# The opening of a decoder-layer kernel: smaller first pieces on two DMA queues, another warming operand, and five additions on another engine

## The chip, the cores and the metric

The kernel runs on one core of a Trainium2 chip. The metric is device time in microseconds (us) for one execution. The core has TensorE (PE, with its weight loads shown apart as PEld), VectorE (DVE), ScalarE (ACT), GpSimd (POOL) and SyncE (SP), which here only issues DMAs. Its DMAs are moved by 16 DMA engines.

## The reference

One decoder layer on x of 1024 tokens by 1024 features, in float32. What matters for the change is the head of it:

```python
h = rms_norm(x, norm1_w[l])
proj = h @ w_in[l]
da_q, da_k, da_v, dn_qkv, dn_z, dn_a, dn_b = jnp.split(proj, [SPLIT_1, ..., SPLIT_6], axis=-1)
```

`rms_norm` divides each token by the root of its mean square and multiplies with a weight per feature. The columns of `proj` feed a differential attention and a gated delta rule, which run in parallel over the same tokens. Their outputs are concatenated, projected and added to x, and a squared-ReLU MLP with its own norm follows.

## The kernel before, in words

A float32 product is made of three products of rounded parts. Each operand is split into a part H, rounded to a shorter mantissa, and the rest L = value - H. A product is then H·H + H·L + L·H, on one PSUM bank. ACT makes the H parts and DVE the L parts.

**The first stage** computes 520 columns of `proj` (the gate columns z, with a and b) and needs the whole of x. x lies in `x_cols`, feature by feature: block `k` (of `KB` = 8) has 128 features on the partitions and 1024 tokens. The stage walks over k. For every k it multiplies each of `NT` = 8 token blocks `tb` with 260 weight columns (`UC`), in three terms "h", "l" and "m", so 24 matmuls of 128x260 for each k, into eight PSUM banks `zb`. The weights of this first half (called unit 1) come as four raw pieces of two k each (`wraw`, loaded by `z_weights`). After the walk, `second(tb)` makes the other 260 columns (unit 0) and PE goes on to the next projections.

The work of each k, by name and line of the kernel before:

- `load_x` (L288) loads block k of x into `xt`, five buffers deep; `z_weights` (L280) loads a raw weight piece. All go through SP's queue, in an order that the code writes out, and the ninth DMA and each later one waits until the DMA eight places before it has landed.
- `x_round` (L302, ACT) makes `hH` from `xt` times the norm weights `n1c` (a small load, L275); `x_rest` (L305, DVE) makes `hL`.
- `z_round` (L309, ACT) makes `wH` of a weight piece; `z_rest` (L313, DVE) makes `wL`.
- `square` (L340, ACT) squares block k, and `add_square` (L343, DVE) adds it to `ssum_` (`xsum` in the trace), from which the norm factors follow. Squares use three buffers (`nsq`).
- `z_mm` issues the matmuls: L320 is "h", L322 "l", L324 "m".

The norm factor of a token is only applied after the products, so the matmuls needn't wait for the sums of squares. PE reads them at L402, after `second(0)`: 8 float32 products of `ssum_` with the tile `ones`.

**What sets the order.** In this stage the order on PE, DVE and ACT is that of the code (a manual schedule): k by k. Behind it only PE's order is fixed, and a scheduler places the rest. Ahead of the first data, PE runs `WARM` = 19 transposes of the identity `ident` (L351), which GpSimd builds with a memset and a select (masks.py:197 and 199). Their results are not used.

Of the kernel before, what the change touches and what calls it, by code (L numbers as in the profile page):

```python
# [9 lines left out]
F32 = mybir.dt.float32  # L10
# [3 lines left out]
ALU = mybir.AluOpType  # L14
# [4 lines left out]
P = 128  # L19
# [9 lines left out]
UC = 260  # L29


WARM = 19
MARGIN = 0.25
MIX_T = 8000.0
MIX_A = 3400.0
# [82 lines left out]
def tile_hymba_layer(  # L118
# [6 lines left out]
    nc = tc.nc  # L125
# [97 lines left out]
    V.memset(neghalf, -0.5)  # L223
    poshalf = const.tile([P, 4], F32, name="poshalf")
    V.memset(poshalf, 0.5)

    def rstd(o, ss, scale, eps, pool, tag, n):
        t = pool.tile([P, n], F32, tag=tag, name=tag) if pool else laid(tag)
# [42 lines left out]
    v4 = lambda t: t.rearrange("p (c d) -> p c d", d=P)  # L271
    ones = n1.tile([P, P], F32, name="ones")
    V.memset(ones, 1.0)
    n1c = n1.tile([P, KB], F32, name="n1c")
    nc.sync.dma_start(n1c, n1_cols)  # L275
    xts, wz = [], [[[staged(t).rearrange("p (k c) -> p k c", k=KB) for t in ("wH", "wL")], []] for _ in range(2)][::-1]

    def z_weights(u, i):
        raw = n2.tile([P, 2 * UC], F32, tag="wraw", name="wraw", bufs=8).rearrange("p (k c) -> p k c", k=2)
        last = nc.sync.dma_start(raw, w_in_v[:, 2 * i:2 * i + 2, 3072 + UC * u:3072 + UC * (u + 1)])  # L280
        wz[u][1].append(raw)
        return last

    def load_x(k, cuts=(slice(0, 1024),)):
        if cuts[0].start == 0:
            xts.append(n2.tile([P, SEQ], F32, tag="xt", name="xt", bufs=5))
        for c in cuts:
            nc.sync.dma_start(xts[k][:, c], x_cols[k, :, c])  # L288

    cut = (slice(0, 512), slice(512, 1024))  # L290
    load_x(0, cut[:1])
    z_weights(1, 0)
    load_x(0, cut[1:])
    for k in range(1, KB):
        load_x(k)
        if k in (1, 3, 5):
            z_weights(1, (k + 1) // 2)
    for i in range(4):
# [5 lines left out]
    def x_rest(k, c):  # L304
        V.scalar_tensor_tensor(hL[:, k, c], xts[k][:, c], n1c[:, k:k + 1], hH[:, k, c].bitcast(F32),  # L305
                               ALU.mult, ALU.subtract)

    def z_round(u, i):
        S.copy(wz[u][0][0][:, 2 * i:2 * i + 2], wz[u][1][i])  # L309

    def z_rest(u, i):
        wh, wl = [x[:, 2 * i:2 * i + 2] for x in wz[u][0]]
        V.tensor_tensor(wl, wz[u][1][i], wh.bitcast(F32), ALU.subtract)  # L313

    def z_mm(ps, u, tb, k, terms="hlm"):
        (wh, wl), _ = wz[u]
        sl = slice(tb * P, (tb + 1) * P)
        for t in terms:
            if t == "h":
                T.matmul(ps[:, :UC], hH[:, k, sl], wh[:, k, :], start=(k == 0), stop=False)  # L320
            elif t == "l":
                T.matmul(ps[:, :UC], hH[:, k, sl], wl[:, k, :], start=False, stop=False)  # L322
            else:
                T.matmul(ps[:, :UC], hL[:, k, sl], wh[:, k, :], start=False, stop=(k == KB - 1))  # L324
# [13 lines left out]
    def square(k):  # L338
        sqs[k] = n2.tile([P, SEQ], F32, tag="nsq", name="nsq", bufs=3) if k else ssum_
        S.activation(sqs[k], xts[k], AF.Square)  # L340

    def add_square(k):
        V.tensor_tensor(ssum_, ssum_, sqs[k], ALU.add)  # L343

    with tc.manual_schedule(engines={T.engine, V.engine, S.engine}):
        zb = [pool.tile([P, 512], F32, tag=tag, name="ps_z")
              for pool, tag in ((pj, "pj"), (ph, "ph"), (pm, "pm"), (pt_, "pt")) for _ in range(2)]
        first_table = n1.tile([P, 1], F32, name="first_table")
        S.activation(first_table, neghalf[:, 0:1], AF.Tanh)
        for i in range(WARM):  # L350
            T.transpose(zb[7][:, :P], ident, ident)  # L351
        for c in cut:
            x_round(0, c)
            if c.start == 0:
                z_round(1, 0)
        x_rest(0, cut[0])
        z_rest(1, 0)
        x_rest(0, cut[1])
        for t in "hlm":
            for tb in range(NT):  # L360
                z_mm(zb[tb], 1, tb, 0, t)
        square(0)
        for k in range(1, KB):
            x_round(k, full)
            if k % 2 and k < 7:
                z_round(1, (k + 1) // 2)
            elif k in (6, 7):
                z_round(0, k - 6)
            square(k)
            x_rest(k, full)  # L370
            if k % 2 and k < 7:
                z_rest(1, (k + 1) // 2)
            elif k in (6, 7):
                z_rest(0, k - 6)
            if 1 < k < 6:
# [12 lines left out]

    tail = zb[7]
# [1418 lines left out]
```

## Time and profile before

| what | value |
|---|---|
| median of 3 runs | 1230.07 us (1228.01 to 1232.25) |
| profiled execution, its time | 1229.3 us |
| its span (first to last record) | 1227.6 us |
| PE busy | 1211.4 us, 99% |
| DVE busy | 844.4 us, 69% |
| ACT busy | 609.9 us, 50% |
| GpSimd busy | 122.8 us, 10% |

A row of the timeline gives the start in us from the span's start, the duration in us, the engine, the line, the operation, what is written and read with its shape, and how often; brackets hold the idle time just before on that engine and what ended it. Several rows of one kind in a run are merged (x4). A matmul's end is modelled, and successive ones overlap: the spacing of starts says how fast PE goes. Sizes of DMAs are in KB of 1024 bytes.

### The profile page before, as it was taken

What the parts mean: (1) busy time and instruction counts of PE and PEld (TensorE: products, weight loads), DVE (VectorE), ACT (ScalarE), POOL (GpSimd) and SP (SyncE); (2) the same over time, 40 slices, a digit from 0 to 9 for tenths busy, and PEclk for the clock granted to TensorE, in tenths of its full rate; (3) what the DMA queues carried; (4) which work ended last, traced back from release to release, by engine and by line L of the source; (5) the groups of instructions that cost most, each with busy time, mean ns of one, the idle gap of its engine ahead of it and who ended that gap; (6) DMA issues with size and microseconds to landing.
All of it is one profiled execution on the core that took longest, in us unless ns stands there. A gap on an engine that the chain in (4) does not pass through costs nothing.

```text
span 1227.6 us, 17618 instructions
## 1 busy us (share of the span) xinstructions
PE 1211.4 (99%) x6331; PEld 1027.0 (84%) x6331; DVE 844.4 (69%) x1437; ACT 609.9 (50%) x1181; POOL 122.8 (10%) x162
## 2 busy tenths in 40 slices
PE   9999999999899999999999999999999999999998
PEld 9978888898788878888788888888888888888887
DVE  7686788477867567766798554565577955786553
ACT  8465545245567555656566444454563333333331
POOL 0011110223332331212100000000000000000000
PEclk9999999999999999999999999999999999999999
DMA  6554342457755674334528433443279855433301
GB/s 230 180 169 134 110 131 86 117 180 225 234 155 165 194 236 140 109 86 144 181 87 280 158 127 138 172 172 137 103 248 351 324 187 183 164 103 104 137 35 69
DMA packets 160784, 199.04 MB, mean 162 GB/s; under 512 B 20961, under 2 KB 120633, under 8 KB 160697
## 3 DMA queue, kind: packets, MB, share of 16 engines
q1 hardware_dynamic: 160696, 197.92, 49.0%
q8 instruction: 50, 0.82, 0.3%
q14 instruction: 38, 0.30, 0.1%
HBM read 132.32 MB, written 65.56 MB: 161 GB/s over the span
## 4 chain that ended last, share of the span: by engine, by line
PE 87%; DVE 4%; DMA 4%; ACT 2%; issue 2%; POOL 0%; SPq 0%; ACTq 0%; DVEq 0%; POOLq 0%
PE X L1406 5%; PE X L1405 5%; PE X L1407 5%; PE X L1723 4%; PE X L1721 4%; PE X L1722 4%; PE ps_dn L204 3%; PE ps_dn L206 3%; PE ps_dn L205 3%; PE Y L1406 3%; PE Y L1405 3%; PE Y L1407 3%; PE ps_qk L974 2%; PE ps_qk L976 2%; PE ps_qk L975 2%; PE Z L1723 2%
## 5 line engine op out<-in xcount | busy, mean ns | idle before, releaser
L1324 ACT CAST hH<-ur 128x1024 fp32r<-128x1024 f32 x56 | 58.7, 1050 | 166.0 <-PE X L1722 79.7
L1325 DVE TENSOR_TENSOR hL<-ur,hH 128x1024 fp32r<-128x1024 f32 x56 | 68.4, 1222 | 79.1 <-ACT hH L1324 79.0
L1325 DVE TENSOR_TENSOR op<-raw,op 128x1024 fp32r<-128x1024 f32 x48 | 58.7, 1223 | 75.7 <-PE X L1406 42.3
L1721 PE MATMUL X<-hH 128*128 128x512 f32 x224 | 87.1, 389 | 0.0
L1722 PE MATMUL X<-hL,hH 128*128 128x512 f32 x224 | 87.1, 389 | 0.0
L1723 PE MATMUL X<-hH,hL 128*128 128x512 f32 x224 | 87.1, 389 | 0.0
L974 PE MATMUL ps_qk<-wH,hH 128*128 128x512 f32 x192 | 81.2, 423 | 0.0
L204 PE MATMUL ps_dn<-hH,wH 128*128 128x512 f32 x192 | 76.0, 396 | 0.0
L205 PE MATMUL ps_dn<-hL,wH 128*128 128x512 f32 x192 | 75.6, 394 | 0.0
L976 PE MATMUL ps_qk<-wH,hL 128*128 128x512 f32 x192 | 75.5, 393 | 0.0
L206 PE MATMUL ps_dn<-hH,wL 128*128 128x512 f32 x192 | 75.4, 393 | 0.0
L975 PE MATMUL ps_qk<-wL,hH 128*128 128x512 f32 x192 | 75.1, 391 | 0.0
L1325 DVE TENSOR_TENSOR hL<-dw,hH 128x1024 fp32r<-128x1024 f32 x56 | 68.1, 1217 | 3.2 <-ACT hH L1324 3.2
L1324 ACT CAST op<-raw 128x1024 fp32r<-128x1024 f32 x48 | 50.5, 1052 | 34.7 <-PE Y L1407 20.1
L1324 ACT CAST hH<-dw 128x1024 fp32r<-128x1024 f32 x56 | 58.6, 1047 | 16.7 <-DMA dw<-in_w_down_dram 5.2
L1116 ACT ACTIVATE pexp<-ps_sc,mx 128x128 f32<-128x128 f32 (+7 forms) x64 | 47.3, 742 | 27.4 <-DVE mx L1112 27.3
L562 DVE SCALAR_TENSOR_TENSOR cy<-cp,pv,cy 128x512 f32<-128x512 f32 x72 | 53.8, 748 | 8.7 <-ACT cy L560 7.8
L1112 DVE TENSOR_REDUCE mx<-ps_sc 128x1 f32<-128x128 f32 (+7 forms) x64 | 47.7, 753 | 13.7 <-PE ps_sc L1110 13.0
L1244 PE MATMUL ps_op<-wH,hH 128*128 128x512 f32 x128 | 53.6, 419 | 0.0
L198 ACT CAST wH<-wraw 128x512 fp32r<-128x512 f32 x64 | 37.1, 623 | 27.6 <-DMA wraw<-in_w_in_dram 17.4
L1246 PE MATMUL ps_op<-wH,hL 128*128 128x512 f32 x128 | 50.4, 393 | 0.0
L1245 PE MATMUL ps_op<-wL,hH 128*128 128x512 f32 x128 | 50.0, 391 | 0.0
(355 smaller groups left out, 3391.1 us busy)
## 6 DMA issues: line engine op xcount, KB each, us to landing
ur<-ud SPq DMA_DIRECT2D x28, 1024.0 KB, 4.9
raw<-in_w_up_dram SPq DMA_DIRECT2D x32, 512.0 KB, 3.8
dw<-in_w_down_dram SPq DMA_DIRECT2D x32, 512.0 KB, 7.3
qk_d<-qa SPq DMA_DIRECT2D x32, 256.0 KB, 3.2
ud<-ua SPq DMA_DIRECT2D x16, 512.0 KB, 4.0
ud<-s SPq DMA_DIRECT2D x16, 512.0 KB, 2.7
wraw<-in_w_in_dram SPq DMA_DIRECT2D x24, 256.0 KB, 3.6
wraw<-in_w_in_dram SPq DMA_DIRECT2D x48, 128.0 KB, 2.6
```

The costliest lines, as they stand in the source:

```text
L204: T.matmul(ps, lh(k), rh(k), start=(k == 0), stop=False)
L205: T.matmul(ps, lh(k), rl(k), start=False, stop=False)
L206: T.matmul(ps, ll(k), rh(k), start=False, stop=(k == n - 1))
L974: T.matmul(ps, hH[:, 4 * kh + k, sl], wh[:, k, :], start=(kh + k == 0), stop=False)
L975: T.matmul(ps, hH[:, 4 * kh + k, sl], wl[:, k, :], start=False, stop=False)
L976: T.matmul(ps, hL[:, 4 * kh + k, sl], wh[:, k, :], start=False, stop=(kh + k == 4))
L1324: S.copy(dst[0], src)
L1325: V.tensor_tensor(dst[1], src, dst[0].bitcast(F32), ALU.subtract)
L1405: T.matmul(ps, op[0][:, k, cs], h[0][:, k, :], start=start and k == 0, stop=False, skip_group_check=True)
L1721: T.matmul(o, v[0][:, j, sl], v[2][:, j, c], start=s0, stop=False, skip_group_check=True)
L1722: T.matmul(o, v[0][:, j, sl], v[3][:, j, c], start=False, stop=False, skip_group_check=True)
L1723: T.matmul(o, v[1][:, j, sl], v[2][:, j, c], start=False, stop=s1, skip_group_check=True)
```

## The change

1. The first block of x comes as pieces of 256, 256 and 512 columns in place of two of 512; the second block comes as two of 512 in place of one of 1024. `n1c` is issued after the first piece of x in place of ahead of it.
2. The first raw weight piece (two k) is loaded as two halves of one k each. The half for k = 0 is issued by ACT's queue, ahead of ACT's other work, and the half for k = 1 by SP, behind both halves of x's second block. Rounding and rest of this piece are split in the same way.
3. PE's products before the data are 9 float32 matmuls of `ones` with itself, in place of 19 transposes of `ident`. `ones` is DVE's first memset; the memsets of `neghalf` and `poshalf` come behind it.
4. Of the additions of squares, those of blocks 1 to 5 go to GpSimd, and 6 and 7 stay on DVE, behind the walk.

```diff
-WARM = 19
+WARM = 9
...
     neghalf = const.tile([P, 32], F32, name="neghalf")
-    V.memset(neghalf, -0.5)
     poshalf = const.tile([P, 4], F32, name="poshalf")
-    V.memset(poshalf, 0.5)
...
     V.memset(ones, 1.0)
+    V.memset(neghalf, -0.5)
+    V.memset(poshalf, 0.5)
     n1c = n1.tile([P, KB], F32, name="n1c")
-    nc.sync.dma_start(n1c, n1_cols)
...
-    cut = (slice(0, 512), slice(512, 1024))
+    cut = (slice(0, 256), slice(256, 512), slice(512, 1024))
     load_x(0, cut[:1])
-    z_weights(1, 0)
+    first_raw = n2.tile([P, 2 * UC], F32, tag="wraw", name="wraw", bufs=8).rearrange("p (k c) -> p k c", k=2)
+    wz[1][1].append(first_raw)
+    nc.scalar.dma_start(first_raw[:, 0], w_in_v[:, 0, 3072 + UC:3072 + 2 * UC])
+    nc.sync.dma_start(n1c, n1_cols)
     load_x(0, cut[1:])
+    load_x(1, (slice(0, 512), slice(512, 1024)))
+    nc.sync.dma_start(first_raw[:, 1], w_in_v[:, 1, 3072 + UC:3072 + 2 * UC])
     for k in range(1, KB):
-        load_x(k)
+        if k > 1:
+            load_x(k)
...
-    def z_round(u, i):
-        S.copy(wz[u][0][0][:, 2 * i:2 * i + 2], wz[u][1][i])
+    def z_round(u, i, ks=slice(0, 2)):
+        S.copy(wz[u][0][0][:, 2 * i:2 * i + 2][:, ks], wz[u][1][i][:, ks])
...
     def add_square(k):
-        V.tensor_tensor(ssum_, ssum_, sqs[k], ALU.add)
+        (G if k < 6 else V).tensor_tensor(ssum_, ssum_, sqs[k], ALU.add)
...
         for i in range(WARM):
-            T.transpose(zb[7][:, :P], ident, ident)
+            T.matmul(zb[7][:, :P], ones, ones, start=True, stop=True)
         for c in cut:
             x_round(0, c)
             if c.start == 0:
-                z_round(1, 0)
-        x_rest(0, cut[0])
-        z_rest(1, 0)
-        x_rest(0, cut[1])
+                z_round(1, 0, slice(0, 1))
+        z_rest(1, 0, slice(0, 1))
+        for c in cut:
+            x_rest(0, c)
         for t in "hlm":
             for tb in range(NT):
                 z_mm(zb[tb], 1, tb, 0, t)
+        half = (slice(0, 512), slice(512, 1024))
+        for c in half:
+            x_round(1, c)
+            if c.start == 0:
+                z_round(1, 0, slice(1, 2))
         square(0)
         for k in range(1, KB):
-            x_round(k, full)
+            if k > 1:
+                x_round(k, full)
...
             square(k)
-            x_rest(k, full)
+            if k > 1:
+                x_rest(k, full)
+            else:
+                x_rest(1, half[0])
+                z_rest(1, 0, slice(1, 2))
+                x_rest(1, half[1])
...
-            if 1 < k < 6:
+            if 1 < k < 7:
                 add_square(k - 1)
...
-        for k in (5, 6, 7):
+        for k in (6, 7):
             add_square(k)
```

The order of PE's instructions changes in one row only, the products before the data. Three other places move. The first is ACT's queue from the program's start to the rounding of block 2. In these rows 128x520 is a weight piece for two k and 128x260 for one; `xsum` and `nsq` are written by `square`. Before:

```order
L349 ACT_TABLE_LOAD
L349 ACTIVATE first_table<-neghalf 128x1
L302 ACTIVATE hH<-xt,n1c 128x512
L309 CAST wH_76<-wraw 128x520
L302 ACTIVATE hH<-xt,n1c 128x512
L340 ACTIVATE xsum<-xt 128x1024
L302 ACTIVATE hH<-xt,n1c 128x1024
L309 CAST wH_76<-wraw 128x520
L340 ACTIVATE nsq<-xt 128x1024
```

and with the change:

```order
L293 DMA wraw<-in_w_in_dram 128x260
L354 ACT_TABLE_LOAD
L354 ACTIVATE first_table<-neghalf 128x1
L307 ACTIVATE hH<-xt,n1c 128x256
L314 CAST wH_76<-wraw 128x260
L307 ACTIVATE hH<-xt,n1c 128x256
L307 ACTIVATE hH<-xt,n1c 128x512 x2
L314 CAST wH_76<-wraw 128x260
L307 ACTIVATE hH<-xt,n1c 128x512
L345 ACTIVATE xsum<-xt 128x1024
L314 CAST wH_76<-wraw 128x520
L345 ACTIVATE nsq<-xt 128x1024
```

In both, the rounding of block 2 (128x1024) stands right behind the square of block 1 (the first `nsq`). The first square (`xsum`) stood between the two blocks of x, ahead of the rounding of block 1; it now stands behind that rounding and behind the second weight half.

The second place is SP's queue at the program's start, each row one DMA, with what it waits for (DMAHW are the completions of earlier DMAs). Before:

```order
L275 DMA n1c<-in_n_cols_dram 128x8
L288 DMA xt<-in_x_cols_dram 128x512
L280 DMA wraw<-in_w_in_dram 128x2x260
L288 DMA xt<-in_x_cols_dram 128x512
L288 DMA xt<-in_x_cols_dram 128x1024
L280 DMA wraw<-in_w_in_dram 128x2x260
L288 DMA xt<-in_x_cols_dram 128x1024 x2
L280 DMA wraw<-in_w_in_dram 128x2x260 [waits DMAHW0_49]
```

and with the change:

```order
L287 DMA xt<-in_x_cols_dram 128x256
L294 DMA n1c<-in_n_cols_dram 128x8
L287 DMA xt<-in_x_cols_dram 128x256
L287 DMA xt<-in_x_cols_dram 128x512 x3
L297 DMA wraw<-in_w_in_dram 128x260
L279 DMA wraw<-in_w_in_dram 128x2x260 [waits DMAHW0_49]
L287 DMA xt<-in_x_cols_dram 128x1024 [waits DMAHW1_49]
L287 DMA xt<-in_x_cols_dram 128x1024 [waits DMAHW2_49]
```

The weight half for k = 1 is now the seventh DMA of SP, behind all of blocks 0 and 1 of x, and the first DMA that waits for a completion is the one behind it.

The third place is GpSimd, between its constants (`tri`, `after`, `blk`) and the norm factors (`rt`), with the change:

```order
L433 AFFINE_SELECT tri<-ones 128x128
L267 AFFINE_SELECT after<-after 128x128
L552 AFFINE_SELECT blk<-blk 128x128
L348 TENSOR_TENSOR xsum<-xsum,nsq 128x1024 x5
L422 TENSOR_TENSOR rt<-nrt,neghalf 128x8
```

Before, `rt` follows `blk` directly. DVE has five additions fewer in the walk or behind it, and the squares of blocks 4 to 7 on ACT wait for GpSimd's additions, which give their buffers free, where they waited for DVE's.

More of the change, by code (lines that the diff above doesn't have):

```diff
@@ L306, in x_rest, with z_rest @@
                                ALU.mult, ALU.subtract)
-    def z_round(u, i):
[L309 to L313, printed above, removed]
+    def z_round(u, i, ks=slice(0, 2)):
+        S.copy(wz[u][0][0][:, 2 * i:2 * i + 2][:, ks], wz[u][1][i][:, ks])
+    def z_rest(u, i, ks=slice(0, 2)):
+        wh, wl = [x[:, 2 * i:2 * i + 2][:, ks] for x in wz[u][0]]
+        V.tensor_tensor(wl, wz[u][1][i][:, ks], wh.bitcast(F32), ALU.subtract)
     def z_mm(ps, u, tb, k, terms="hlm"):
```

## The prediction

> **What bounds the kernel now.** I read the page's busy times first, then the chain of waits and the timeline of the first 13 us, because all that the change edits runs before 33 us.
>
> ```profile
> span 1227.6 us, 17618 instructions
> PE 1211.4 (99%) x6331; PEld 1027.0 (84%) x6331; DVE 844.4 (69%) x1437; ACT 609.9 (50%) x1181; POOL 122.8 (10%) x162
> ...
> 12.00:16.00 4.00, 4.00 (x36) 4.00 (x35) 3.81 (x4) 4.00 (x6) 0.00 (x0) 1.00 1.05 378
> 16.00:20.00 4.00, 4.00 (x36) 4.00 (x35) 4.00 (x5) 4.00 (x5) 0.00 (x0) 1.00 1.05 356
> ```
>
> PE is busy for 99% of the span, and the stages from 12 to 20 us (their columns: stretch, length, PE, PEld, DVE, ACT, GpSimd, clock, DMA share, GB/s) show it full. So the change can only move the time at which PE begins to run without a gap. The chain of waits names that point (start, duration, what):
>
> ```profile
> 2.70 5.77 DMA xt<-in_x_cols_dram
> 8.49 1.16 ACT hH L302
> 9.70 0.39 PE ps_z L320
> ```
>
> Block 1 of x lands at 8.49, ACT rounds it, PE starts k = 1 at 9.70 and does not stop again in this stage. The timeline gives PE's side of it:
>
> ```profile
> 1.68 4.32 PE L351 MATMUL ps_z<-ident 128*128 128x128 f32 x19 [1.68 <-POOL ident masks.py:199]
> 5.86 0.76 PE L320 MATMUL ps_z<-wH,hH 128*128 128x260 f32 x4
> 6.92 0.75 PE L320 MATMUL ps_z<-wH,hH 128*128 128x260 f32 x4 [0.29 <-ACT hH L302]
> 8.46 1.12 PE L324 MATMUL ps_z<-wH,hL 128*128 128x260 f32 x8
> 11.72 1.12 PE L324 MATMUL ps_z<-wH,hL 128*128 128x260 f32 x8
> 12.68 0.28 PE L320 MATMUL ps_z<-wH,hH 128*128 128x260 f32 x1
> ```
>
> Starts in full flow are 0.12 us apart ((12.68 - 11.72) / 8), so a k of 24 matmuls takes 2.88 us. Products of k = 2 begin at 12.68. **That is the number to beat**: an earlier start of k = 0 is worth nothing unless k = 2 starts earlier too. All that PE could win is the wait ahead of 5.86 and the two gaps before 9.70.
>
> **ACT's queue.** It feeds each k, and its rows show what stands ahead of k = 2:
>
> ```profile
> 4.06 0.72 ACT L302 ACTIVATE hH<-xt,n1c 128x512 fp32r<-128x512 f32 x1 [1.76 <-DMA xt<-in_x_cols_dram]
> 5.18 0.63 ACT L309 CAST wH<-wraw 128x520 fp32r<-128x520 f32 x1 [0.40 <-DMA wraw<-in_w_in_dram]
> 6.14 0.72 ACT L302 ACTIVATE hH<-xt,n1c 128x512 fp32r<-128x512 f32 x1 [0.33 <-DMA xt<-in_x_cols_dram]
> 6.77 1.04 ACT L340 ACTIVATE xsum<-xt 128x1024 f32<-128x1024 f32 x1
> 8.49 1.15 ACT L302 ACTIVATE hH<-xt,n1c 128x1024 fp32r<-128x1024 f32 x1 [0.67 <-DMA xt<-in_x_cols_dram]
> 9.55 0.61 ACT L309 CAST wH<-wraw 128x520 fp32r<-128x520 f32 x1
> 10.06 1.06 ACT L340 ACTIVATE nsq<-xt 128x1024 f32<-128x1024 f32 x1
> 11.03 1.13 ACT L302 ACTIVATE hH<-xt,n1c 128x1024 fp32r<-128x1024 f32 x1
> ```
>
> The square of block 0 (6.77) runs inside the wait for block 1, so it is free. The rounding of block 2 ends at 12.16, half a microsecond before PE needs it. ACT is thus nearly the bound already.
>
> **The change, part by part.**
>
> *PE before the data.* `ones` is ready after one memset of DVE, where `ident` waits for two GpSimd instructions:
>
> ```profile
> 0.88 0.09 DVE L223 MEMSET neghalf<- 128x32 f32 x1 [0.88 <-PEq L1790]
> 0.96 0.17 DVE L273 MEMSET ones<- 128x128 f32 x1
> 32.81 1.84 PE L402 MATMUL ps_z<-ones,xsum 128*128 128x2 f32 x16
> 97.63 0.60 PE L599 MATMUL ps_t<-ident,q 128*128 128x128 f32 x4
> 98.07 1.06 PE L606 MATMUL ps_m<-q,k 128*128 128x128 f32 x8
> ```
>
> PE starts at about 0.88 + 0.17 + 0.06 = 1.11 in place of 1.68. The 8 float32 products of L402 are 16 records, so 9 become 18. The last record of a row takes some 0.27 us, so four transposes in 0.60 us are 0.11 apart, and so are the halves of L606 ((1.06 - 0.28) / 7). The 19 first transposes are (4.32 - 0.42) / 18 = 0.217 apart, twice that: PE runs them at half speed, though the clock column says 1.00. The 18 halves at half speed end at 1.11 + 18 x 0.217 = 5.0; at full speed they would end at 3.1. I take 5.0, since the transposes were slow to their last. They then hold PE until 5.0 even if data is there. The Trainium skill ("TensorE: Matmul & The Clock Gate", Part 1) says that the array starts at half rate and is released after about 3.4 us of busy time, by a window that does not start with the kernel. By that rule the release could come up to 3.4 us later than seen in some executions, of either kernel. In the kernel before, 9 matmuls at half speed behind 6.92 would push k = 1 by some 0.6 us; with the change, the slack ahead of k = 2 (below) covers it. One trace can't show how often.
>
> *First pieces.* Issue and landing:
>
> ```profile
> 0.81 0.39 SPq L275 DMA_DIRECT2D n1c<-in_n_cols_dram  x1
> 1.25 0.42 SPq L288 DMA_DIRECT2D xt<-in_x_cols_dram  x1
> 1.72 0.43 SPq L280 DMA_DIRECT2D wraw<-in_w_in_dram  x1
> ...
> n1c<-in_n_cols_dram SPq DMA_DIRECT2D x1, 4.0 KB, 1.6
> ...
> 2.00:3.00 1.00, 1.00 (x6) 1.00 (x5) 0.00 (x0) 0.28 (x2) 0.40 (x2) 1.00 0.68 154
> 3.00:4.00 1.00, 1.00 (x7) 1.00 (x6) 0.00 (x0) 0.00 (x0) 0.00 (x0) 1.00 0.94 286
> ```
>
> The first piece took 4.06 - 1.25 = 2.81 us to land, the tiny `n1c` 1.6. So the piece issued at 0.81 lands between 2.4 and 3.6, the weight half from ACT too; I take 3.5. A rounding of 512 columns takes 0.72 and of 1024 1.13, so 256 take 0.5 and the half weight piece 0.4: PE has data at about 4.4. It starts at 5.0, behind its warming products, 0.9 earlier than now. ACT's own DMA issue (0.4) and the later memset of `neghalf` (0.1) lie in the 1.76 us that ACT idles ahead of 4.06. The skill ("DMA: Bandwidth & Descriptors", Issuing engines are not separate DMA queues) says that a second issuing engine saves only issue time. By that the second queue saves one issue, about 0.4 us, and no transfer; no trace of the kernel before has a second queue.
>
> *What k = 1 and k = 2 wait for.* The DMA engines are full from 3 us on (0.94), so order and bytes decide. 154 of 286 GB/s in the second from 2 to 3 put the first bytes at 2.46, 1.2 after the issue. Before, block 1 lands with 4 + 512 + 260 + 512 = 1288 KB issued up to it. Now the weight half for k = 1 is the last of the same 1288 KB. The stream begins one issue earlier (0.81 for 1.25), so I put its landing at 8.49 - 0.44 = 8.05. Bounds: 8.5, if the earlier issue buys nothing; and 1288 KB at 286 GB/s from 2.0 (first issue plus 1.2) is 6.6, with the 0.7 by which the first 256 KB lagged behind this rate (4.06 against 2.46 + 0.92): 7.3.
>
> From that landing, starts on ACT follow each other by 0.30 (half cast, from 0.51), 0.63 (512 columns), 0.97 (square of block 0, now behind the wait), 0.51 (cast), 0.97 (square of block 1), and 1.13 to the end of block 2's rounding, then 0.15 to PE's flow: 4.66 us. So k = 2 flows at 8.05 + 4.66 = **12.71**, against 12.68: no gain. With the bounds it is 11.96 to 13.16, that is 0.7 earlier to 0.5 later. PE itself would be ready sooner: k = 0 from 5.0, a wait for the third x piece to about 5.9 (landing near 5.1, rounding 0.72), 20 more matmuls to 8.3, the wL half, 24 matmuls: 11.5. This 1.2 us becomes a new wait of PE ahead of k = 2, and it is the cover for a slow clock. Later roundings have room: each k asks ACT for about 2.5 us (16.57 to 19.07 in the rows of ACT) against PE's 2.88, as before.
>
> *The additions.*
>
> ```profile
> 16.57 1.04 ACT L340 ACTIVATE nsq<-xt 128x1024 f32<-128x1024 f32 x1
> 19.07 1.05 ACT L340 ACTIVATE nsq<-xt 128x1024 f32<-128x1024 f32 x1
> 28.11 1.21 DVE L343 TENSOR_TENSOR xsum<-xsum,nsq 128x1024 f32<-128x1024 f32 x1
> 30.61 1.22 DVE L343 TENSOR_TENSOR xsum<-xsum,nsq 128x1024 f32<-128x1024 f32 x1
> L199 POOL TENSOR_TENSOR wL<-wraw,wH 128x512 fp32r<-128x512 f32 x12 | 15.4, 1296 | 15.8 <-ACT wH L198 14.5 <-PE ps_sc L1110 1.2
> ```
>
> GpSimd has 1.296 us for 512 columns, so 2.6 for 1024, twice DVE's 1.22. Five from the end of block 1's square (about 8.05 + 3.4 = 11.5) end at 24.5. DVE's last two then end near 28.2 + 2 x 1.22 = 30.6, and PE reads the sum at 32.81, about a second after DVE finishes it now (31.83). The squares wait for freed buffers: the seventh needs the fourth addition (21.9), and runs at 25. The cover is PE's own work until 32.81. DVE is relieved of 6.1 us but bounds nothing here, so that buys nothing.
>
> **Sum**: 1229.3 (the profiled execution, span 1227.6) + 0.03 = 1229.3; the median of the runs shown lies 0.8 above it, so about **1230.0**. PE's order behind the stage is unchanged, so a shift of k = 2 goes through to the end at most one to one.
>
> **Rivals.**
>
> 1. *The pieces land early.* If the weight half lands by 6.8, ACT is no longer last and PE's own 11.5 decides: 1.2 us less, 1228.8. For it: less is queued behind each piece. Against it: the engines are full, and the bytes ahead are the same.
> 2. *Small pieces move slower.* Four pieces where two were, rows of 1 KB and 2 KB; a landing at 9.0 puts k = 2 at 13.66, 1.0 later: 1231.0. Against it: 516 KB in 2 KB and 1 KB rows took 2.08 us (4.06 to 6.14), 512 KB in long rows 2.35 (6.14 to 8.49).
> 3. *GpSimd becomes the bound.* PE must wait at L402 once an addition takes over (32.8 - 2.4 - 11.5) / 5 = 3.8 us. At 5.2, double the row's price because DVE reads the same memory at the same time, the sum is ready at 11.5 + 26 + 2.4 = 39.9: 7.1 us later, 1237. Against it: the twelve GpSimd subtractions average 1296 ns, and DVE is busy for 69% of the span.
>
> **How the numbers follow.** My forecast, k = 2 within 0.7 of now, has 0.65; rival 1 0.15; rival 2 0.15; rival 3 0.03; the rest 0.02. Less than 0.3% (3.7 us) can't be told from no change here. Only rival 3 leaves that band by itself; runs spread over 4.2 us, so I leave 0.05 to faster and 0.06 to slower, and 0.89 between. The first two rivals and the spread of a median (about 1 us to each side) give 1227.6 to 1232.
>
> **What would show it.** Right: first x pieces rounded from about 3.5, PE on data near 5.0, ACT waiting for the second weight half until near 8, PE idle about a microsecond ahead of k = 2, and k = 2 near 12.7. Wrong, if k = 2 starts before 11.9 or after 13.2, if GpSimd's additions take over 3.8 us each, or if PE waits at the sums.

## The result, and the profile after

| | median us (range, runs) |
|---|---|
| kernel before | 1229.24 (1227.6 to 1232.25, 8) |
| changed kernel | 1234.28 (1232.51 to 1236.43, 8) |

The changed kernel takes 1.0039 times as long, with a 95% interval of 1.0028 to 1.005: it is slower by some 4.8 us, more than the 0.3% that counts as no change here. The forecast was 1230.0 us, with 0.06 for slower. Its profiled execution took 1234.74 us.

The head of the page, and five stretches of the timeline's busy times (columns as in the prediction):

```profile
span 1233.0 us, 17627 instructions
PE 1212.5 (98%) x6330; PEld 1027.9 (83%) x6330; DVE 850.5 (69%) x1435; ACT 609.9 (49%) x1184; POOL 137.5 (11%) x167
...
12.00:16.00 4.00, 3.05 (x23) 2.63 (x22) 2.85 (x2) 4.00 (x6) 3.76 (x2) 1.00 1.08 373
16.00:20.00 4.00, 3.78 (x32) 3.57 (x31) 4.00 (x2) 4.00 (x5) 3.92 (x2) 1.00 1.06 388
20.00:24.00 4.00, 2.44 (x19) 2.02 (x17) 4.00 (x2) 3.47 (x5) 3.92 (x2) 1.00 0.24 76
24.00:28.00 4.00, 2.84 (x23) 2.84 (x24) 4.00 (x2) 3.90 (x7) 3.29 (x2) 1.00 0.55 122
28.00:32.00 4.00, 3.78 (x32) 3.57 (x31) 4.00 (x9) 0.20 (x1) 0.00 (x0) 1.00 0.07 23
```

DVE's busy time did not fall by the 6.1 us of the five additions; it rose from 844.4 to 850.5. PE, full from 12 to 20 us before, now idles 0.95 + 0.22 + 1.56 + 1.16 + 0.22 = 4.1 us between 12 and 32. The waits view of the changed kernel says for what, between 6 and 60 us (columns: PE's line, what it waited for, us in total, times, longest):

```profile
PE ps_z L329 <- DVE hL L310: 2.0, 4, 1.3
PE ps_z L327 <- DVE wL L318: 1.5, 1, 1.5
PE ps_z L325 <- ACT hH L307: 0.8, 2, 0.6
```

3.5 of 4.3 us are waits for the rests that DVE makes (one short wait, of 0.2 for `hH`, came at 6.70, ahead of these stretches). DVE's timeline:

```profile
15.55 3.42 DVE L310 SCALAR_TENSOR_TENSOR hL<-xt,n1c,hH 128x1024 fp32r<-128x1024 f32 x1
18.90 2.87 DVE L318 TENSOR_TENSOR wL<-wraw,wH 128x520 fp32r<-128x520 f32 x1
21.69 6.77 DVE L310 SCALAR_TENSOR_TENSOR hL<-xt,n1c,hH 128x1024 fp32r<-128x1024 f32 x2
28.38 0.69 DVE L318 TENSOR_TENSOR wL<-wraw,wH 128x520 fp32r<-128x520 f32 x1
28.99 1.27 DVE L310 SCALAR_TENSOR_TENSOR hL<-xt,n1c,hH 128x1024 fp32r<-128x1024 f32 x1
```

and GpSimd's:

```profile
12.16 15.20 POOL L348 TENSOR_TENSOR xsum<-xsum,nsq 128x1024 f32<-128x1024 f32 x5 [9.77 <-ACT nsq L345]
```

While GpSimd adds, from 12.16 to 27.36, a rest of x takes DVE 3.4 us and a weight rest 2.87. After 28.4 the same instructions take 1.27 and 0.69 again. The kernel before has these two groups:

```profile
L305 DVE SCALAR_TENSOR_TENSOR hL<-xt,n1c,hH 128x1024 fp32r<-128x1024 f32 x7 | 9.0, 1280 | 2.6 <-ACT hH L302 2.6
L313 DVE TENSOR_TENSOR wL<-wraw,wH 128x520 fp32r<-128x520 f32 x8 | 5.4, 692 | 0.3 <-ACT wH L309 0.3
```

So four rests of x and one weight rest have grown, all but the first of them by about the same 2.1 to 2.2 us, whatever their own length (the first rest, at 13.15, took 2.48). The loss goes through to the end: the factor's first instruction on DVE behind the sums (`nrt`) starts at 40.16 in the changed kernel and at 34.69 before, 5.5 us apart, and the spans are 5.4 apart:

```profile
40.16 0.17 DVE L421 TENSOR_SCALAR nrt<-ps_z 128x8 f32<-128x8 f32 x1 [2.08 <-PE ps_z L418]
```

```profile
34.69 0.17 DVE L405 TENSOR_SCALAR nrt<-ps_z 128x8 f32<-128x8 f32 x1 [1.65 <-PE ps_z L402]
```

The 4.3 us of waits don't make 5.4 by themselves. A stop costs PE some 0.26 us more than its idle time: a matmul's row (0.28) is 0.16 longer than the spacing (0.12), and the second start behind a stop comes 0.22 after the first. Counted from the last eight products of k = 0 (8.24 us; 8.46 before), the six stops from 13.17 on cost 4.1 + 6 x 0.26 = 5.7 us, and a shorter one at 9.54 another 0.3. The kernel before has one of 0.4 at 9.70, and it was 0.2 behind at the start: 5.7 + 0.3 - 0.4 - 0.2 = 5.4.

The front of the program went nearly as forecast. PE's and ACT's timelines:

```profile
1.12 4.21 PE L356 MATMUL ps_z<-ones 128*128 128x128 f32 x18 [1.12 <-DVE poshalf L273]
4.98 1.50 PE L325 MATMUL ps_z<-wH,hH 128*128 128x260 f32 x4
13.17 0.39 PE L325 MATMUL ps_z<-wH,hH 128*128 128x260 f32 x1 [0.62 <-ACT hH L307]
```

```profile
4.00 0.51 ACT L307 ACTIVATE hH<-xt,n1c 128x256 fp32r<-128x256 f32 x1 [1.27 <-DMA n1c<-in_n_cols_dram]
8.62 0.41 ACT L314 CAST wH<-wraw 128x260 fp32r<-128x260 f32 x1 [1.30 <-DMA wraw<-in_w_in_dram]
```

The second weight half is taken up at 8.62, and k = 2 begins 4.55 later at 13.17, half a microsecond after the 12.68 of before.

### The profile page after: what moved, and what is told of

Its sections match the earlier page's. It is cut to its first block, busy times and chain, and to the rows that moved or that the text cites. A ratio compares the mean times of both kernels' runs of the same rounds, so it can differ in the third digit from the quotient of the medians.

```text
span 1233.0 us, 17627 instructions
## 1 busy us (share of the span) xinstructions
PE 1212.5 (98%) x6330; PEld 1027.9 (83%) x6330; DVE 850.5 (69%) x1435; ACT 609.9 (49%) x1184; POOL 137.5 (11%) x167
## 4 chain that ended last, share of the span: by engine, by line
PE 84%; DMA 6%; DVE 5%; ACT 2%; issue 1%; SPq 1%; POOL 0%; ACTq 0%; DVEq 0%; POOLq 0%
PE X L1422 5%; PE X L1423 5%; PE X L1421 5%; PE X L1737 4%; PE X L1739 4%; PE X L1738 4%; PE ps_dn L204 3%; PE ps_dn L206 3%; PE ps_dn L205 3%; PE ps_qk L990 3%; PE Y L1422 3%; PE Y L1423 3%; PE Y L1421 2%; PE ps_qk L992 2%; PE ps_qk L991 2%; PE Z L1737 2%
```

## The experiments

Ratios are to the kernel before, with 95% intervals; behind a time stands the number of runs. Line numbers shift by a few from kernel to kernel, but names don't.

**Which part costs it.** First the changed kernel with the additions back on DVE (e1), then the kernel before with the additions alone (e2). In e1 the fifth addition stays within the walk; the kernel before has it behind the walk.

```diff
-        (G if k < 6 else V).tensor_tensor(ssum_, ssum_, sqs[k], ALU.add)
+        V.tensor_tensor(ssum_, ssum_, sqs[k], ALU.add)
```

> The changed kernel with only the five additions moved back to VectorE. Theory A (GpSimd's additions slow VectorE's two-input instructions while both run): VectorE's 1024-column rests return from about 3.4 to 1.28 us, PE stops waiting for hL and wL; what is left is the front end, where block 2 was rounded by 13.11 in place of 12.16, so k = 2 is about 0.6 us later than in the kernel before: 1229.8 us, ratio 1.0005. Rival B (the smaller pieces, the second queue and the new warming products cost the 5 us): still near 1234.

Measured: 1230.23 us (11), 1.0011 [1.0002, 1.002].

```diff
 (kernel before)
-        V.tensor_tensor(ssum_, ssum_, sqs[k], ALU.add)
+        (G if k < 6 else V).tensor_tensor(ssum_, ssum_, sqs[k], ALU.add)
...
-            if 1 < k < 6:
+            if 1 < k < 7:
                 add_square(k - 1)
...
-        for k in (5, 6, 7):
+        for k in (6, 7):
             add_square(k)
```

> The kernel before with only the five additions of squares on GpSimd. Theory A: nearly the whole loss, 4.0 to 5.0 us, so 1233.2 to 1234.2, with VectorE's 1024-column rests near 3.4 us from about 11 to 26 us. Rival B: no loss, 1229.2.

Measured: 1234.58 us (4), 1.0041 [1.0026, 1.0056]. DVE's rests of x in this kernel:

```profile
L305 DVE SCALAR_TENSOR_TENSOR hL<-xt,n1c,hH 128x1024 fp32r<-128x1024 f32 x7 | 16.6, 2400 | 2.5 <-ACT hH L302 2.5
```

The additions alone make the whole loss, and in e1, without them, DVE's rests are back at 1278 ns. The loss comes down to this one expression. It divides differently here: in e2's profiled execution PE waited only 2.1 us, and the granted clock was 0.66 and 0.91 in the two stretches of 4 us from 20 on, which cost some 1.3 us (2.77 x 0.34 + 3.86 x 0.09, by PE's busy time there).

**Is it GpSimd's work as such, or what it reads?** In e3 GpSimd copies each square over the sum in place of adding it: the same buffers, waits and releases, with one input less. The sums of squares are left out.

```diff
-        (G if k < 6 else V).tensor_tensor(ssum_, ssum_, sqs[k], ALU.add)
+        if k < 6:
+            G.tensor_copy(ssum_, sqs[k])
+        else:
+            V.tensor_tensor(ssum_, ssum_, sqs[k], ALU.add)
```

> The changed kernel with GpSimd copying each of the squares 1 to 5 over the sum (one input) in place of adding it (two inputs); the sum of squares is left out. If any GpSimd access holds VectorE up, a rest that overlaps a copy grows by the copy's overlap (some 1 to 1.5 us each, five times) and the loss shrinks to about 1 to 2 us: 1230.5. If only two-input GpSimd instructions collide, VectorE's rests stay at 1.28 us and the time is that of the additions moved back, 1229.8. Rival B: 1234.

Measured: 1230.03 us (10), 1.0007 [0.9998, 1.0016]. The groups, and one meeting of the two engines:

```profile
L310 DVE SCALAR_TENSOR_TENSOR hL<-xt,n1c,hH 128x1024 fp32r<-128x1024 f32 x6 | 7.8, 1296 | 4.8 <-ACT hH L307 4.8
L349 POOL COPY xsum<-nsq 128x1024 f32<-128x1024 f32 x5 | 5.8, 1170 | 13.9 <-ACT nsq L345 13.9
```

```profile
16.03 1.23 POOL L349 COPY xsum<-nsq 128x1024 f32<-128x1024 f32 x1 [1.37 <-ACT nsq L345]
```

```profile
16.97 1.36 DVE L310 SCALAR_TENSOR_TENSOR hL<-xt,n1c,hH 128x1024 fp32r<-128x1024 f32 x1 [0.62 <-ACT hH L307]
```

With copies in place of additions the loss is gone. So it is not the move to another engine, nor the order of waits, but the addition itself on GpSimd beside DVE. That copies never hold DVE up (1296 against 1280 ns) isn't shown: being shorter, they lie beside DVE's rests for only 1.8 of their 5.8 us. Where a rest began with 0.29 us of a copy still to run (16.97), it took 0.08 us more than undisturbed; the copies that began under a DVE instruction took 1.14 to 1.23 us, against 1.04 for the first.

**Contention without a dependence on GpSimd's result.** In e5 the kernel before keeps its additions on DVE, and GpSimd adds the same squares into an unused tile as well.

```diff
 (kernel before)
         V.tensor_tensor(ssum_, ssum_, sqs[k], ALU.add)
+        if k < 6:
+            G.tensor_tensor(rB, rB if k > 1 else sqs[k], sqs[k], ALU.add)
```

> The kernel before, unchanged in its own work, with five further additions on GpSimd: at each of the squares 1 to 5 it adds the square into a tile that is not yet in use. VectorE keeps its additions and waits for nothing that GpSimd makes. Theory A (both engines slow each other while each reads two inputs from SBUF): VectorE's rests grow to about 3.4 us in the overlap as in the changed kernel, and its own additions too; more work lies in the overlap, so the time is above the changed kernel's: 1236 to 1240. Rival C (VectorE lost its time by waiting for GpSimd's sums and buffers, not by being slowed): 1229.4.

Measured: 1238.22 us (4), 1.0067 [1.0052, 1.0082]. DVE's timeline and GpSimd's:

```profile
13.93 3.44 DVE L343 TENSOR_TENSOR xsum<-xsum,nsq 128x1024 f32<-128x1024 f32 x1
...
23.36 1.21 DVE L343 TENSOR_TENSOR xsum<-xsum,nsq 128x1024 f32<-128x1024 f32 x1
```

```profile
10.80 2.13 POOL L345 TENSOR_TENSOR rB<-nsq 128x1024 f32<-128x1024 f32 x1 [8.40 <-ACT nsq L340]
13.00 9.88 POOL L345 TENSOR_TENSOR rB<-rB,nsq 128x1024 f32<-128x1024 f32 x3
25.87 3.29 POOL L345 TENSOR_TENSOR rB<-rB,nsq 128x1024 f32<-128x1024 f32 x1 [2.99 <-ACT nsq L340]
```

No instruction of the first stage reads GpSimd's tile (only the squares' buffers are held until GpSimd has read them too), and yet DVE's addition takes 3.44 us at 13.93, where GpSimd adds, and 1.21 at 23.36, where GpSimd is idle (22.88 to 25.87). GpSimd's own first addition took 2.13 us, hardly held up by DVE, and those under DVE's work 3.3. The Trainium skill ("GPSIMD Engine Reference", §1 Specifications) says that GpSimd shares its interfaces to the on-chip memory with VectorE, with contention for DVE instructions in a two-port mode or with two inputs from that memory. That agrees in kind with e2 and e5, where the DVE instructions held up have two inputs; e3's few meetings don't decide it for copies.

**Only DVE's instructions with two inputs?** In e8 the rest of x is made from one input. The subtraction of `hH` is left out.

```diff
-        V.scalar_tensor_tensor(hL[:, k, c], xts[k][:, c], n1c[:, k:k + 1], hH[:, k, c].bitcast(F32),
-                               ALU.mult, ALU.subtract)
+        V.tensor_scalar(hL[:, k, c], xts[k][:, c], n1c[:, k:k + 1], None, ALU.mult)
```

> The changed kernel, GpSimd's additions kept, with VectorE's rest of x made from one SBUF input (x times the norm weight) in place of two; the subtraction of the rounded part is left out. The weights' rests keep two inputs. Theory A1 (only two-input instructions of VectorE collide with two-input ones of GpSimd): the one-input rests take the same time inside the overlap as behind it (some 0.6 to 1.2 us), the weights' rests of 0.69 us still grow where they overlap, and the time is near that of the additions moved back, 1230. Theory A2 (any SBUF read of VectorE collides): the one-input rests grow two- to threefold in the overlap and the time lies between 1231 and 1234.

Measured: 1230.97 us (8), 1.0009 [0.9996, 1.0023]. The timeline of DVE:

```profile
17.22 5.70 DVE L310 TENSOR_SCALAR hL<-xt,n1c 128x1024 fp32r<-128x1024 f32 x2
22.84 2.88 DVE L317 TENSOR_TENSOR wL<-wraw,wH 128x520 fp32r<-128x520 f32 x1
25.64 0.74 DVE L310 TENSOR_SCALAR hL<-xt,n1c 128x1024 fp32r<-128x1024 f32 x1
```

One input is held up too: 0.74 us alone, 2.85 in the overlap, again 2.1 more. The theory that two inputs on both sides are needed falls. Whether this instruction, which takes 0.74 us where the two-input one takes 1.28, works in a two-port mode isn't shown. The time is nearly that of before all the same, since the turns are shorter: a pair of one GpSimd addition and one rest takes (22.84 - 17.22) / 2 = 2.81 us, and PE, which needs such a rest every 2.88 us, lost only 2.0 us in waits.

**The price by the number of additions.** In e6 two additions stay on GpSimd, three go back.

```diff
-        (G if k < 6 else V).tensor_tensor(ssum_, ssum_, sqs[k], ALU.add)
+        (G if k < 3 else V).tensor_tensor(ssum_, ssum_, sqs[k], ALU.add)
```

> The changed kernel with only the additions of squares 1 and 2 on GpSimd, those of 3 to 7 on VectorE. Theory A: about 6 us of overlap in place of 15, in which VectorE loses about 3.7 us, and its three further additions take 3.7 us of the idle time that could have absorbed that; the loss against the kernel before is 1 to 3.5 us: 1230.5 to 1233, between the additions moved back (1230.2) and the changed kernel (1234.3). Rival C: 1230.2.

Measured: 1231.77 us (10), 1.0018 [1.0008, 1.0028]: between e1 and the changed kernel. Two rests grow, and then DVE works off its delay.

**What is left without the additions.** e11 is the kernel before with the new warming products, the new order of DVE's memsets and the fifth addition within the walk (on DVE); the diff below shows the products alone. e12 is e1 with the old 19 transposes, so the pieces, queues and orders of the front, again with the fifth addition within the walk.

```diff
 (e11: kernel before)
-WARM = 19
+WARM = 9
...
-            T.transpose(zb[7][:, :P], ident, ident)
+            T.matmul(zb[7][:, :P], ones, ones, start=True, stop=True)
 (e12: changed kernel, additions on VectorE)
-WARM = 9
+WARM = 19
...
-            T.matmul(zb[7][:, :P], ones, ones, start=True, stop=True)
+            T.transpose(zb[7][:, :P], ident, ident)
```

> The kernel before with only the new warming products (9 of the ones in place of 19 transposes) and, as in the run with the additions moved back, the fifth addition within the walk on VectorE. PE's warming ends near 5.3 in place of 6.0, and the first data come at 5.2 to 5.9 as before, so by theory A this costs nothing: 1229.2 to 1229.6, with k = 2 flowing near 12.7. If the products release the clock later than the transposes do, the matmuls of k = 0 are 0.24 us apart for longer, and k = 1, which has no slack in this order, comes up to 1.3 us later: 1230 to 1230.5.

> The run with the additions moved back, with the old 19 transposes in place of the 9 products: the pieces alone. They put the rounding of block 2 some 0.8 us later (11.8 to 13.0 against 11.03 to 12.16): if the pieces are what is left of the loss, 1229.8 to 1230.2, ratio 1.0005 to 1.0011; if it is the warming products, 1229.3.

Measured: e11 1230.18 us (11), 1.0000 [0.999, 1.001]; e12 1231.21 us (11), 1.0012 [1.0001, 1.0022]. The warming products change nothing. e12 costs about 1.5 us, just separable from nothing, but its profiled execution doesn't show that as a late start. PE's and DVE's timelines:

```profile
12.28 0.39 PE L325 MATMUL ps_z<-wH,hH 128*128 128x260 f32 x1 [0.17 <-ACT hH L307]
...
28.57 0.39 PE L329 MATMUL ps_z<-wH,hL 128*128 128x260 f32 x1 [1.43 <-DVE hL L310]
```

```profile
25.77 0.29 DVE L455 TENSOR_TENSOR lamp<-lamt 128x128 f32<-128x128 f32 x1 [1.07 <-DMA lamt<-in_lambda_k_dram]
```

Here k = 2 begins 0.4 us ahead of the kernel before (12.68), and PE waits 1.43 us at the end of the walk, for the rest of block 7. On DVE that rest (27.24) stands behind the fifth addition (26.11), and both behind an instruction that waited 1.07 us for a small load. So what the pieces cost by themselves, without that addition in the walk, isn't shown. The 1.5 us also don't add to the 5.0 of the additions alone (4.8 in all); that they are hidden where PE waits for DVE anyway is likely, but not shown.

**Mending the front.** In e7, which has all additions on DVE, the later weight half is requested ahead of the second half of x's block 1, the square of block 0 runs ahead of that half's rounding, while ACT waits for it, and the square of block 1 gives way to the rounding of block 2.

```diff
-    load_x(1, (slice(0, 512), slice(512, 1024)))
+    load_x(1, (slice(0, 512),))
     nc.sync.dma_start(first_raw[:, 1], w_in_v[:, 1, 3072 + UC:3072 + 2 * UC])
+    load_x(1, (slice(512, 1024),))
...
             if c.start == 0:
+                square(0)
                 z_round(1, 0, slice(1, 2))
-        square(0)
...
-            square(k)
+            if k == 2:
+                square(1)
+            if k > 1:
+                square(k)
```

> The changed kernel with the additions on VectorE, the second weight half issued ahead of the second half of block 1, the square of block 0 ahead of that weight half's rounding on ScalarE, and the square of block 1 behind the rounding of block 2. Theory A with my model of ScalarE's queue: block 2 rounded near 11.0 to 11.9 in place of 13.11, PE limited by its own 11.7, k = 2 flowing 0.7 to 1.0 us earlier than in the kernel before: 1228.4, ratio 0.9993. If the smaller pieces are no gain at all: 1229.2 or later.

Measured: 1229.33 us (11), 1.0002 [0.9993, 1.0011]. k = 2 starts at 12.58, 0.6 before the changed kernel's, and PE then waits 0.8 us for the rest of block 7 at 27, behind the fifth addition on DVE. e9 moves that addition behind the walk; e10 puts additions 5 and 6 between the rest of block 7 and the last weight rests, and 7 behind the walk.

```diff
 (e9, against e7)
-            if 1 < k < 7:
+            if 1 < k < 6:
...
-        for k in (6, 7):
+        for k in (5, 6, 7):
 (e10, against e7)
-            if 1 < k < 7:
+            if 1 < k < 6:
                 add_square(k - 1)
+            elif k == 7:
+                add_square(5)
+                add_square(6)
...
-        for k in (6, 7):
+        for k in (7,):
```

> The reordered front end of the run before, with the fifth addition again behind the walk, as in the kernel before, so that VectorE makes block 7's rest about 1.2 us earlier. There PE waited 0.9 us for it, and the copies of the results began at 28.74 in place of 27.60. If that wait is what ate the gain: copies from about 27.6, and 1228.4 to 1228.9 us, ratio 0.9993 to 0.9997. If the front end holds no gain: 1229.3 or more.

> The reordered front end again, with the additions of squares 5 and 6 between block 7's rest and the last two weight rests, so that only the seventh stands behind the walk. In the run with the fifth addition behind the walk, the last addition came behind two unrelated instructions on VectorE and PE waited 1.1 us for the sums. Here block 7's rest is as early, the sums are ready near 32.3, and neither wait should be there: k = 2 flows near 12.0, the copies begin near 27.6, 1228.4 to 1229.0. If VectorE's total work bounds the stage, PE waits about as long at another instruction, and the time stays at 1229.3 or above.

Measured: e9 1232.03 us (11), 1.0021 [1.0012, 1.0031]; e10 1228.34 us (12), 0.9994 [0.9984, 1.0004]. In e9 the wait for block 7 went, but two weight rests of the next stage were scheduled ahead of the last addition, and PE waited 1.1 us at the sums; its granted clock was then 0.61 from 36 to 40 us (1.00 from 32 to 36), which cost another 1.6 us. In e10 both waits are gone (0.3 us is left, for ACT). It is the fastest kernel of the study and can't be told from the one before. So what the front could win is below 0.2%.

**Turns, or a shared bandwidth?** In e13 each GpSimd addition of the changed kernel is cut into four of 256 columns: the same bytes in shorter instructions. e14 does the same in e7.

```diff
-        (G if k < 6 else V).tensor_tensor(ssum_, ssum_, sqs[k], ALU.add)
+        if k < 6:
+            for q in range(4):
+                c = slice(q * 256, q * 256 + 256)
+                G.tensor_tensor(ssum_[:, c], ssum_[:, c], sqs[k][:, c], ALU.add)
+        else:
+            V.tensor_tensor(ssum_, ssum_, sqs[k], ALU.add)
```

> The changed kernel with each of the five GpSimd additions cut into four of 256 columns; everything else is the changed kernel's. Theory 'turns by whole instructions': a VectorE instruction that meets GpSimd's additions waits for one instruction of GpSimd, so with quarters for some 0.55 to 0.65 us (2.1 / 4, with a little overhead) instead of 2.1. VectorE's rests of x under the additions take 1.8 to 2.0 us instead of 3.4, TensorE's waits for hL and wL in the walk shrink to under 0.5 us, and the time is 1230 to 1231, next to the kernel that has the additions back on VectorE (1230.2). Rival 'shared bandwidth': the two engines share the same bytes per second, whatever the length of an instruction; the rests stay at 3 to 3.4 us, the waits at some 3.5 us, the time at 1234.

> The kernel with the later weight half requested earlier and the first sums' order mended (the label e7_front, additions on VectorE, 1229.3), with the additions of blocks 1 to 5 on GpSimd in quarters of 256 columns. Theory 'turns by whole instructions': VectorE is relieved of 6 us of additions for five holds-up of some 0.6 us, so TensorE's wait of 0.8 us for the rest of block 7 goes: 1228.0 to 1229.5. Rival 'shared bandwidth': the rests take over 3 us as in the changed kernel, 1233 or more.

Measured: e13 1232.49 us (5), 1.0036 [1.0023, 1.0049]; e14 1234.87 us (5), 1.0053 [1.0039, 1.0067]. The times miss what the turns should have given, and e14's lies where the rival had it, yet the mechanism is there. In e14 too the rests average 1506 ns and not over 3 us; PE waited 1.8 us for roundings, 1.9 for a rest and 1.1 at the sums, and its clock was at about half from 40 to 43 us. The groups of e13 between 8 and 36 us:

```profile
L310 DVE SCALAR_TENSOR_TENSOR hL<-xt,n1c,hH 128x1024 fp32r<-128x1024 f32 x6 | 8.7, 1454 | 5.0 <-ACT hH L307 3.3 <-DMA lamt<-in_lambda_k_dram 1.6
...
L351 POOL TENSOR_TENSOR xsum<-xsum,nsq 128x256 f32<-128x256 f32 x20 | 22.7, 1173 | 8.9 <-ACT nsq L345 8.9
```

```profile
15.49 1.24 DVE L318 TENSOR_TENSOR wL<-wraw,wH 128x520 fp32r<-128x520 f32 x1
```

Rests of x average 1454 ns (2400 in e2, 1280 undisturbed), and the longest hold-up was of a weight rest, from 0.69 to 1.24 us; a quarter alone takes GpSimd 0.73. So DVE is held up for no more than a quarter. Now GpSimd pays: the twenty take 22.7 us, 4.5 for each block in place of 3.0, where 20 x 0.73 alone would be 14.6. Hence a new wait, on ACT, whose squares need the buffers that GpSimd frees:

```profile
21.43 1.06 ACT L345 ACTIVATE nsq<-xt 128x1024 f32<-128x1024 f32 x1 [1.51 <-POOL xsum L351]
...
25.67 1.06 ACT L345 ACTIVATE nsq<-xt 128x1024 f32<-128x1024 f32 x1 [1.62 <-POOL xsum L351]
```

The roundings stand behind these squares in ACT's order. PE waited 0.9 us for the last of them (another 0.6 is the front's own wait ahead of k = 2) and 1.0 for a rest, and then came a second price, in the windows of one microsecond:

```profile
27.00:28.00 1.00, 0.18 (x1) 0.18 (x2) 0.47 (x4) 1.00 (x2) 1.00 (x2) 1.00 0.82 286
28.00:29.00 1.00, 0.33 (x2) 0.11 (x2) 1.00 (x1) 0.28 (x1) 1.00 (x2) 1.00 0.00 0
29.00:30.00 1.00, 0.64 (x5) 0.65 (x6) 1.00 (x2) 0.07 (x1) 1.00 (x2) 1.00 0.00 0
30.00:31.00 1.00, 1.00 (x7) 1.00 (x7) 0.45 (x1) 1.00 (x2) 1.00 (x1) 0.50 0.00 0
...
33.00:34.00 1.00, 1.00 (x9) 1.00 (x9) 0.44 (x1) 1.00 (x6) 1.00 (x1) 0.79 0.06 16
```

After three microseconds with PE busy for 0.18 + 0.33 + 0.64 = 1.15 of them, the granted clock falls to 0.50 for about 3.4 us, in which PE does about half the work: 1.5 to 1.7 us lost. Without that, e13 would have come to about 1230.9, within its expectation; this is worked out from one profiled execution, and what the clock did in the others isn't shown. The Trainium skill ("TensorE: Matmul & The Clock Gate", Part 1) gives a window of 3413 ns, and half rate after at least one idle window. The length at half rate agrees; that the window must be idle doesn't, since PE was busy for over a third of these three microseconds.

**Following the wait.** e15 is e13 with a fourth buffer for squares, and six for raw weight pieces in place of eight to make room. e16 is e15 with four additions on GpSimd and three on DVE behind the walk.

```diff
 (e15, against e13)
-... tag="wraw", name="wraw", bufs=8)
+... tag="wraw", name="wraw", bufs=6)
...
-        sqs[k] = n2.tile([P, SEQ], F32, tag="nsq", name="nsq", bufs=3) if k else ssum_
+        sqs[k] = n2.tile([P, SEQ], F32, tag="nsq", name="nsq", bufs=4) if k else ssum_
 (e16, against e15)
-        if k < 6:
+        if k < 5:
...
-            if 1 < k < 7:
+            if 1 < k < 6:
...
-        for k in (6, 7):
+        for k in (5, 6, 7):
```

> The changed kernel with the five additions in quarters (as e13_quarters) and with four buffers for squares in place of three; to make room, the raw weight pieces have six buffers in place of eight. Theory 'the wait moved to the ring of squares': with quarters VectorE is held up little (its rests mean 1454 ns), but GpSimd takes 4.5 us per block, the squares on ScalarE wait 1.5 us each for freed buffers, and the roundings behind them come late. With a fourth buffer the squares of blocks 5 and 6 wait no longer, so TensorE's 1.5 us of waits for hH in the walk goes. The last addition still ends near 34 and VectorE's two near 36.5, so TensorE, then some 2 us earlier, waits for the sums instead: 1231.5 to 1232.5, little better than the quarters alone. Rival 'the late roundings come from something else' (ScalarE's own load or the DMAs): the waits for hH stay, and no wait for the sums appears, 1232.5.

> As e15_quarters_buffers, with the additions of blocks 1 to 4 alone on GpSimd and those of 5, 6 and 7 on VectorE behind the walk. By the same theory the four end near 29.5, VectorE's three behind the walk near 34, about when TensorE comes to the sums: the waits in the walk and at the sums are both under 1 us, and the time is 1230 to 1231, as with all additions on VectorE (1230.2): the loss is undone, with nothing won. Rival 'any share of additions on GpSimd costs in proportion': four fifths of the changed kernel's loss, 1233.

Measured: e15 1235.9 us (6), 1.0058 [1.0045, 1.007]; e16 1234.05 us (6), 1.0048 [1.003, 1.0066]. Both are slower than expected. The steps of e15 came nearly as the theory has them. ACT copies the banks out from 29.10 on, 3 us earlier than in e13 (32.13; some 1.6 of it is e13's stretch at half rate), and of the 1.5 us for `hH` the front's 0.6 is left, so the ring of squares was what held PE there. PE then waits 2.9 us until DVE is through with the sums. Waits of e15 (named by the last of DVE's instructions it counts, which stands right behind the last addition), and its windows behind:

```profile
PE ps_z L423 <- DVE nlam L466: 2.9, 1, 2.9
```

```profile
37.00:38.00 1.00, 0.57 (x3) 0.60 (x4) 1.00 (x4) 0.00 (x0) 0.00 (x0) 0.54 0.00 0
...
43.00:44.00 1.00, 1.00 (x7) 1.00 (x7) 0.78 (x5) 0.80 (x2) 0.00 (x0) 0.54 0.44 57
```

From 37 to 44 the clock is at about half. That is some 3 us lost, which my expectation had not counted and by which it missed (1235.9 - 3 = 1232.9, against 1231.5 to 1232.5). e16 shows the same with smaller numbers: 1.9 us of wait at the sums, and a granted clock of 0.81 and 0.77 in the 8 us from 36 on, another 1.7 us. Both also moved loads of the next stage in SP's order, through the six buffers, so their times aren't of the additions alone.

## Why the prediction was wrong

**The step that failed** is this sentence: "DVE is relieved of 6.1 us but bounds nothing here, so that buys nothing." It takes the durations of DVE's remaining instructions as given. They were not: with GpSimd's additions beside them, five of them grew, four by some 2.1 us each, and then DVE did bound PE. What was costed at nothing cost 5.0 us (e2).

**Rival 3 had the mechanism and the wrong victim.** It named GpSimd and DVE reading the same memory at the same time, but priced it on GpSimd's additions alone, with a point of decision at 3.8 us each and a wait of PE at the sums. The additions took 3.0 us on average, below that point, and PE did not wait at the sums; the price was paid by DVE's rests in the walk. I gave it 0.03 because "the twelve GpSimd subtractions average 1296 ns, and DVE is busy for 69% of the span". That looked at the wrong engine's rows. The trace of before held the evidence, in DVE's groups of L1126:

```profile
L1126 DVE SCALAR_TENSOR_TENSOR pexp<-pexp,cf 128x256 f32<-128x256 f32 x4 | 3.0, 751 | 0.1
L1126 DVE SCALAR_TENSOR_TENSOR pexp<-pexp,cf 128x384 f32<-128x384 f32 x4 | 2.5, 618 | 0.1
L1126 DVE SCALAR_TENSOR_TENSOR pexp<-pexp,cf 128x128 f32<-128x128 f32 x4 | 1.4, 351 | 0.1
```

256 columns take longer than 384. One of the four fell under one of those twelve subtractions. DVE's and GpSimd's timelines of the kernel before:

```profile
557.84 1.56 DVE L1126 SCALAR_TENSOR_TENSOR pexp<-pexp,cf 128x256 f32<-128x256 f32 x1
```

```profile
556.49 2.62 POOL L199 TENSOR_TENSOR wL<-wraw,wH 128x512 fp32r<-128x512 f32 x2 [2.77 <-ACT wH L198]
```

With 1.07 us more than the 0.49 between its neighbours (351 and 618 ns), this one instruction priced the conflict. There it cost the kernel nothing, because PE wasn't waiting for DVE.

**The price of an addition on GpSimd**, 2.6 us, was too high for one alone (2.13) and too low under DVE's work (2.7 to 3.3). The squares' waits for freed buffers, which were costed at nothing, stayed there.

**The front** was right in its mechanism. PE warmed from 1.12 and took data from 4.98 (1.11 and 5.0 forecast), and ACT waited for the second weight half. ACT took that half up at 8.62 and not at 8.05, just past the bound of 8.5, and the 4.66 us from there to k = 2 measured 4.55. So k = 2 came at 13.17, a hundredth past the bound of 13.16. That is one execution. In the nine profiled kernels with these pieces and queues the half was taken up between 7.73 and 8.62, and k = 2 began between 12.28 (e12) and 13.88 (e1), so the forecast of 12.71 lies within the spread. The first rounding waited until 4.00 for `n1c`, not for x: issued behind the first x piece, these 4 KB took 2.7 us to land, against 1.6 in the kernel before, and the prediction had no term for that. The warming products hid it. e12, at 1.0012, would have stayed in the forecast's band. Rivals 1 and 2 didn't happen as described.

The slack that was to cover a slow clock did not do so in one execution. In the profiled one of e1, PE's products of k = 0 were still at half speed past 9 us:

```profile
8.28 1.94 PE L327 MATMUL ps_z<-wL,hH 128*128 128x260 f32 x8
```

The same eight took 1.11 us from 7.29 on in the changed kernel. In e1 block 2 was rounded by 12.97, and PE came to k = 2 only at 13.88, without a wait.

**The signs named beforehand** did not include the one that appeared: a longer duration of DVE's rests. The list had GpSimd's durations and the sums.

## What to carry to other kernels

Work moved from VectorE to GpSimd is not work taken off VectorE: with GpSimd's additions beside them, the rests and additions of VectorE here lost about the length of a whole GpSimd addition each (2.1 us for 1024 columns), so count the instructions it overlaps before counting the ones it relieves. Before such a move, look in the trace for VectorE instructions that already run beside GpSimd, and compare their durations with their own kind. And a new wait of PE can cost more than its length, where it takes the granted clock to half for some microseconds.

## What the runs showed of the hardware

- **Turns of whole instructions.** DVE and a GpSimd addition take turns: in the changed kernel DVE's starts at 15.55, 18.90 and 21.69 are 3.35 and 2.79 apart, one addition (2.13 alone) plus DVE's own 1.28 or 0.69. In quarters a weight rest that met them grew from 0.69 to 1.24 us, not by 2.1. Equal bytes gave another price, so it isn't a shared bandwidth alone.
- **Fewer inputs.** GpSimd copies of 1024 columns took 1.17 us and left DVE's rests at 1296 ns (e3), with 1.8 us of overlap in all; a longer overlap wasn't tried. An operand less on DVE's side (e8) didn't help.
- **Sources in PSUM.** In the kernel before, a DVE reduction that reads PSUM took 0.94 us under a GpSimd subtraction; its like without one took 0.95. That is one instance, and no run was made for it.
- **The clock falls after short waits that add up.** In e13 waits of 0.88 and 1.03 us within 3 us, in which PE was busy for 1.15, were followed by 3.4 us at half rate. e2 (0.66 from 20 to 24 us) and e5 (0.50 there) show it too. In the profiled execution of the changed kernel, seven waits of 4.3 us in all, spread over 22 us, were not (1.00 throughout). Why one and not the other is open.
